# Mixing one chunk ahead in the output projection, an earlier priority for the last chunks of the FFN, and modulation weights loaded through GpSimd's queue

## The chip, the cores and the metric

The kernel is written in a tile framework for one NeuronCore of a Trainium2 chip. The core has TensorE (matrix products, PE in the profile), VectorE (DVE), ScalarE (ACT), GpSimd (POOL) and SyncE (SP), and 16 DMA engines. Each engine works through its own queue in order. DMAs are started by instructions in the queues of SP, POOL or ACT. The metric is the device time of one execution in microseconds; lower is better.

## The reference

One layer of a diffusion backbone on 1024 tokens of width 1024 with 256 context tokens, all float32:

```python
mod = silu(c) @ w_ada + b_ada                      # 6 x 1024: shift, scale, gate, twice
sh1, sc1, g1, sh2, sc2, g2 = split(mod, 6)
h = modulate(rmsnorm(x, norm1_g), sh1, sc1)
q, k, v, hv, hx1, hx2, gna, ghy = split(h @ w_in)  # 1024 -> 5120
y_na = neighbourhood_attention(q, k, v, k_ctx, v_ctx, rpb)
y_hy = hyena_mixer(hv, hx1, hx2, filters)          # long convolutions through FFTs
m = sigmoid(g_na) * (y_na @ w_na_o) + sigmoid(g_hy) * (y_hy @ w_hy_o)
x = x + g1 * (m @ w_out)
h2 = modulate(rmsnorm(x, norm2_g), sh2, sc2)
x = x + g2 * ((silu(h2 @ w1) * (h2 @ w3)) @ w2)    # hidden width 2816
return rmsnorm(x, final_g)
```

## The kernel before

Products keep float32 accuracy by splitting each operand into a high part in the matmul format (a ScalarE cast) and a low remainder (a VectorE subtraction); `split` (L175 and L176) makes both, and each product is the sum of three: low by high, high by low, high by high. `weights` (L178 to L185) loads a raw weight on SP and splits it.

The program is straight-line. The order of each engine's queue is set when the kernel is built: the framework walks the instructions by priority, which is program order unless a block stands under `high_priority`, and by when it estimates each to be ready. A tile of a pool with `bufs=n` has n places; a load into a place waits until the last reader of the tile that was there before is done.

The stages in order of time, by the names in the trace:

- 0 to 70 us: the early modulation (`ada_early`, L221 to L235), the norm and the turned hidden state `hT`.
- 70 to 280 us: the input projection (`project`, `in_ps`) interleaved with the filters of the Hyena branch and the late modulation. `filters` loads decay tiles `dec` on SP (L359, two places), multiplies them with `filt_ps` on VectorE (L370, `fv`), and transforms them (`dft_ps`, L442 to L444, with matrices `matf` loaded on SP). Spectra go to DRAM by SP (`spec<-ks`, L390) after a ScalarE copy. `ada_rows` (L870 to L921) computes the four late rows of the modulation on VectorE: for each of eight sums of 512 columns it takes eight tiles `wal` of 128x512 (64 loads of 256 KB, four places, L887) and accumulates them into `aacc` (L890, L892); a small matmul `ar_ps` adds over the partitions, and the rows go to DRAM by POOL (`mod<-arow`, L912). POOL's queue also carries the stores of projected tokens (`vtok`, `z`, `hx`, L572) and of projected rows (`qk`, L624), and at the start of each pair of rows eight small loads of the bias (L908).
- 280 to 800 us: the rest of the input projection with the convolutions. 800 to 920 us: attention with the Hyena output (`hyena_out`).
- 920 to 1062 us: `mix`. For each of eight chunks f of the merged channels it loads and splits the attention's output weight `wna[f]`, loads `wout[f]`, multiplies it by g1 and splits it into `wouh` and `woul`, computes `na_ps` for both halves of the tokens (24 matmuls), and on VectorE and ScalarE the gated sum and its split `mh` and `ml` (L1081 to L1084). After every second chunk `rows` (L1096) multiplies the two chunks with their output weights for all eight blocks of tokens (`out_ps`, L1107, 96 matmuls) and adds to the residual. The pool that holds `wouh`, `woul`, `mh` and `ml` has three places for each. The last two chunks are returned, and their `rows` run together with the second norm.
- 1062 to 1490 us: the FFN up, seven products in a Strassen scheme. 1490 to 1712 us: the FFN down, `ffn_down`: seven products of 11 chunks each, in the order 1, 2, 6, 5, 7, 3, 4; each chunk loads a 128x512 tile `ar<-g` (L1316) and splits it and a weight. `close` and `finish` (L1400 to L1431) end each block of the output. In product 4 the last `TAIL` = 3 chunks are multiplied together, block by block.

Of the kernel before, what the change touches and what calls it, by code (L numbers as in the profile page):

```python
# [158 lines left out]
class Block:  # L159
# [712 lines left out]
    def ada_rows(self, pool, psf):  # L872

        nc, a = self.nc, self.a
        ones = pool.tile([P, 32], F32, name="ones", tag="ones", bufs=1)
        nc.gpsimd.memset(ones, 1.0)

        def sums(r, pair):  # L880
            for n, part in enumerate(pair):
                for h in range(2):
                    acc = pool.tile([P, 512], F32, tag="aacc", name="aacc", bufs=2)
                    for k in range(8):
                        w = pool.tile([P, 512], F32, tag="wal2", name="wal", bufs=4)
                        at = part * D + 512 * h
                        nc.sync.dma_start(w, a["w_ada"][k, :, at:at + 512])  # L887
                        c = self.cs[:, 2 * k:2 * k + 1]
                        if k:
                            nc.vector.scalar_tensor_tensor(acc, w, c, acc, op0=ALU.mult, op1=ALU.add)  # L890
                        else:
                            nc.vector.tensor_scalar(acc, w, c, None, op0=ALU.mult)  # L892
                        yield 0.6
                    ps = psf.tile([P, 512], F32, tag="f", name="ar_ps")
                    for j in range(2):
                        g = 64 * h + 32 * j
                        nc.tensor.matmul(ps[g:g + 32, 0:256], ones, acc[:, 256 * j:256 * j + 256], start=True,
                                         stop=True, tile_position=(0, g))
                    rs = r[64 * h:64 * h + 64, 256 * n:256 * n + 256]
                    nc.vector.tensor_add(rs, ps[64 * h:64 * h + 64, 0:256], rs)  # L900

        for pair in ((3, 4), (2, 5)):
            r = pool.tile([P, 512], F32, tag="arow", name="arow", bufs=1)
            nc.gpsimd.memset(r, 0.0)
            for n, part in enumerate(pair):
                for j in range(4):
                    at = part * D + 256 * j
                    nc.gpsimd.dma_start(r[32 * j:32 * j + 1, 256 * n:256 * n + 256], a["b_ada"][0:1, at:at + 256])  # L908
            yield from sums(r, pair)
            for n, part in enumerate(pair):  # L910
                for j in range(4):
                    nc.gpsimd.dma_start(self.modd[part][0:1, 256 * j:256 * j + 256],  # L912
                                        r[32 * j:32 * j + 1, 256 * n:256 * n + 256])
            if pair[0] == 3:
                pt = psf.tile([P, 512], F32, tag="f", name="ada_t")
                for j in range(4):
                    nc.tensor.transpose(pt[:, j * P:(j + 1) * P], r[:, j * P:(j + 1) * P], self.ident)
                v = pt.rearrange("p (n h g q) -> p n q g h", n=2, h=2, g=4)[:, :, 0]
                cols = lambda t: t.rearrange("p (g h) -> p g h", h=2)
                nc.vector.tensor_copy(cols(self.mod2[:, 1, :]), v[:, 0])  # L920
                nc.vector.scalar_tensor_tensor(cols(self.mod2[:, 0, :]), v[:, 1], 1.0, cols(self.ng[:, 1, :]),  # L921
                                               op0=ALU.add, op1=ALU.mult)
# [139 lines left out]
    def mix(self, wp, wo, mp, psf, g1, x1):  # L1062

        nc, a = self.nc, self.a
        gs = []
        for f in range(8):
            wn = self.weights(wo, a["wna"][f], 512)
            raw = wp.tile([P, D], F32, tag="wor4", name="wor", bufs=2)
            nc.sync.dma_start(raw, a["wout"][f])
            nc.vector.tensor_tensor(raw, raw, g1, op=ALU.mult)  # L1070
            w = [mp.tile([P, D], F32R, tag=t, name=t) for t in ("wouh", "woul")]
            self.split(w[0], w[1], raw)
            m = [mp.tile([P, T], F32R, tag=t, name=t) for t in ("mh", "ml")]
            for h in range(2):
                sl = slice(h * 512, (h + 1) * 512)
                ps = psf.tile([P, 512], F32, tag="f", name="na_ps")
                self.gemm(ps, wn, self.ya, 4, 512, h * 512)
                ga = wp.tile([P, 2, 512], F32, tag="gate", name="gate")
                nc.sync.dma_start(ga[:, 0], self.gd[f][:, sl])
                nc.sync.dma_start(ga[:, 1], self.hyd[f][:, sl])  # L1080
                nc.scalar.activation(ga[:, 0], ga[:, 0], AF.Sigmoid)  # L1081
                nc.vector.tensor_tensor(ga[:, 0], ps, ga[:, 0], op=ALU.mult)
                nc.vector.tensor_add(ga[:, 0], ga[:, 0], ga[:, 1])
                self.split(m[0][:, sl], m[1][:, sl], ga[:, 0])  # L1084
            gs.append((m, w))
            if f == 1:
                for j in range(8):
                    nc.sync.dma_start(x1[j], a["x"][j * P:(j + 1) * P, :])
            if f == 7:
                return gs  # L1090
            if len(gs) == 2:
                for j in range(8):
                    self.rows(psf, x1[j], gs, j, "out_ps")
                gs = []

    def rows(self, psf, x1, gs, j, name):  # L1096

# [186 lines left out]
    def ffn_down(self, wa, pool, psf):  # L1284
# [5 lines left out]
        nc, a = self.nc, self.a  # L1290
        N = NH // 2
        AHEAD, TAIL = 4, 3
# [5 lines left out]
        def operand(src, early):  # L1298
            count[0] += not early
            return self.operand(wa if early or count[0] % 8 < 5 else _Bufs(pool, oh=3, ol=3), src)  # L1300

        def load(q, i, pin=True):
            sl = slice(512 * (q % 2), 512 * (q % 2) + 512)
            d = nc.sync.dma_start(w2[i][:, q, :], a["w2"][i + N * (q // 2)][:, sl])
            if pin:
                self.tc.keep_in_program_order(d)

        def product(n, ps, src, start, stop, loads=lambda i: ()):
            rest = []
            for i in range(N):  # L1310
                early = n == 1 and i < AHEAD
                ahead = ExitStack()
                if n != 1 and i == 0:
                    ahead.enter_context(self.tc.high_priority())
                x = wa.tile([P, 512], F32, tag="t", name="ar")
                d = nc.sync.dma_start(x, self.g2d[n][i])  # L1316
                if n == 1 and not early:
                    self.tc.keep_in_program_order(d)
                if early:
                    if i % 2 == 0:  # L1320
                        raw = wa.tile([P, D], F32, tag="wr", name="wr")
                    w = raw[:, 512 * (i % 2):512 * (i % 2) + 512]
                    nc.sync.dma_start(w, a["w2"][i][:, 0:512])
                else:
                    w = src(i)
                if n == 1 and i == AHEAD - 1:
                    for k in range(AHEAD, 2 * AHEAD):
                        load(0, k)
                for q, k, pin in loads(i):
                    load(q, k, pin)  # L1330
                rest.append((operand(x, early), operand(w, early)))
                ahead.close()
                if n == 4 and N - TAIL <= i < N - 1:
                    continue
                for j in range(4):
                    for k, (x, w) in enumerate(rest):
                        for c, (u, v) in enumerate(((1, 0), (0, 1), (0, 0))):
                            nc.tensor.matmul(ps[j], x[u][:, j * P:(j + 1) * P], w[v],  # L1338
                                             start=(start and i == 0 and c == 0),
                                             stop=(stop and i == N - 1 and k == len(rest) - 1 and c == 2),  # L1340
                                             skip_group_check=True)
                    if i == N - 1:
                        yield j
                rest = []
# [32 lines left out]
        for j in product(1, x, b11, True, False, lambda i: ((2, i - AHEAD, True),) if i >= AHEAD else ()):  # L1377
            nc.scalar.copy(c11[j], x[j])
# [6 lines left out]
        for j in product(6, x, t2, False, False):  # L1385
            nc.scalar.copy(c12[j], x[j])
# [83 lines left out]
```

## Time and profile before

| | |
|---|---|
| median of 3 runs | 1712.67 us (1707.35 to 1715.36) |
| the profiled execution | 1714.26 us, of which the span from the first to the last instruction is 1712.2 us |
| TensorE | busy 1655.7 us (97%), 8124 matmuls |
| VectorE | busy 1230.1 us (72%) |
| ScalarE | busy 662.3 us (39%) |
| GpSimd | busy 153.8 us (9%) |
| mean granted TensorE clock | 0.994 |

Busy times are unions of instruction spans. A wait is given as the idle time of an engine just before an instruction, with the instruction or DMA that ended it. A row of the timeline gives the start, the length, the engine (a q behind it stands for its queue), the line, the operation with out<-in, and how many followed each other.

### The profile page before, as it was taken

The page shows a single profiled execution, that of the slowest core. Times are in us where ns is not written, and L with a number is a line of the kernel's source. Part 1 is how long each engine was busy: PE and PEld are TensorE (multiplying, and loading weights), DVE is VectorE, ACT ScalarE, POOL GpSimd, SP SyncE. Part 2 cuts the span into 40 slices and gives each one's busy share as a digit, 9 for nine tenths or more (in the row PEclk, how much of TensorE's full clock was granted, in tenths as well). Part 3 has the DMA queues.
Part 4 walks back from the last instruction along what each step waited for, and adds up shares of the span by engine and source line. Part 5 has one row for each costly group of instructions (what it writes and reads, how often), then busy time and mean ns, then how long its engine had stood idle before and what let it go on. Part 6 is the DMA issues. An engine that isn't in the chain of part 4 may idle for free.

```text
span 1712.2 us, 22620 instructions
## 1 busy us (share of the span) xinstructions
PE 1655.7 (97%) x8124; PEld 1305.4 (76%) x8124; DVE 1230.1 (72%) x2076; ACT 662.3 (39%) x1141; POOL 153.8 (9%) x274
## 2 busy tenths in 40 slices
PE   6999998999999999999999999999999999999997
PEld 2676676777777778887787887888888888878886
DVE  3797586799995966465866868867865566479576
ACT  4611221322222224455654226733333333355455
POOL 0100210100010013020200001010101011100000
PEclk9999999999999999999999999999999999999999
DMA  9286854555463456354757425333433223395344
GB/s 363 101 267 196 272 179 151 203 158 180 156 222 137 138 202 193 104 150 135 215 163 251 140 68 184 123 123 117 156 103 109 95 99 108 106 384 174 99 121 154
DMA packets 114517, 282.48 MB, mean 165 GB/s; under 512 B 15839, under 2 KB 24675, under 8 KB 112101
## 3 DMA queue, kind: packets, MB, share of 16 engines
q1 hardware_dynamic: 94472, 219.99, 38.7%
q0 software_dynamic: 19280, 60.60, 10.5%
q8 instruction: 64, 1.05, 0.3%
q10 hardware_dynamic: 653, 0.44, 0.1%
q14 instruction: 48, 0.39, 0.1%
HBM read 213.60 MB, written 67.39 MB: 164 GB/s over the span
## 4 chain that ended last, share of the span: by engine, by line
PE 66%; issue 8%; DVE 4%; DMA 3%; ACT 1%; POOL 0%; SPq 0%; DVEq 0%; POOLq 0%; ACTq 0%
PE x_ps L1169 15%; PE in_ps L195 13%; PE z_ps L1169 7%; PE dx_ps L1338 5%; PE out_ps L1107 5%; PE dz_ps L1338 3%; PE dft_ps L442 2%; PE hy_ps L195 2%; PE y_ps L1169 2%; PE pt_ps L800 2%; PE pt_ps L786 2%; PE dft_ps L443 1%; PE dft_ps L444 1%; PE dy_ps L1338 1%; PE s_ps L766 1%
## 5 line engine op out<-in xcount | busy, mean ns | idle before, releaser
L195 PE MATMUL in_ps<-hTh,wl 128*128 128x512 f32 x640 | 258.9, 405 | 0.9 <-ACT proj L614 0.5
L195 PE MATMUL in_ps<-hTl,wh 128*128 128x512 f32 x640 | 253.4, 396 | 0.4 <-DVE hTl L176 0.2
L195 PE MATMUL in_ps<-hTh,wh 128*128 128x512 f32 x640 | 253.1, 396 | 0.0
L195 PEld LDWEIGHTS in_ps<-hTh,wl 128*128 128x128 f32 x640 | 121.0, 189 | 31.8 <-issue 5.6
L195 PEld LDWEIGHTS in_ps<-hTl,wh 128*128 128x128 f32 x640 | 121.1, 189 | 27.0 <-DVE hTl L176 1.9
L195 PEld LDWEIGHTS in_ps<-hTh,wh 128*128 128x128 f32 x640 | 121.0, 189 | 26.8 <-issue 0.4
L175 ACT CAST wh<-wr 128x1024 fp32r<-128x1024 f32 (+1 forms) x56 | 51.9, 926 | 140.9 <-PE in_ps L195 110.6
L176 DVE TENSOR_TENSOR wl<-wr,wh 128x1024 fp32r<-128x1024 f32 (+1 forms) x56 | 59.7, 1067 | 62.4 <-ACT wh L175 62.2
L176 DVE TENSOR_TENSOR ol<-ws,oh 128x512 fp32r<-128x512 f32 x88 | 60.4, 688 | 50.2 <-ACT oh L175 50.0
L176 DVE TENSOR_TENSOR ol<-ar,oh 128x512 fp32r<-128x512 f32 x77 | 52.8, 688 | 46.7 <-ACT oh L175 46.7
L175 ACT CAST oh<-ar 128x512 fp32r<-128x512 f32 x77 | 47.9, 622 | 83.5 <-PE dx_ps L1338 33.1
L175 ACT CAST oh<-ws 128x512 fp32r<-128x512 f32 x88 | 54.7, 622 | 56.6 <-PE x_ps L1169 26.5
L442 PE MATMUL dft_ps<-a,matf 128*128 128x512 f32 x128 | 66.3, 599 | 6.3 <-DVE a L430 4.3
L775 ACT ACTIVATE pe<-pe,mx 128x640 f32<-128x640 f32 x64 | 52.6, 822 | 49.1 <-DVE mx L774 49.1
L1338 PE MATMUL dx_ps<-ol,oh 128*128 128x512 f32 x176 | 68.7, 390 | 1.7 <-DVE ol L176 1.7
L774 DVE CUSTOM_DVE_ANT_0 pe<-s_ps,bias 128x640 f32<-128x640 f32 x64 | 50.1, 820 | 28.1 <-PE s_ps L769 28.1
L1338 PE MATMUL dx_ps<-oh,ol 128*128 128x512 f32 x176 | 67.3, 390 | 1.9 <-DVE ol L176 1.9
L1338 PE MATMUL dx_ps<-oh 128*128 128x512 f32 x176 | 68.5, 389 | 0.0
L176 DVE TENSOR_TENSOR ol<-wr,oh 128x512 fp32r<-128x512 f32 x70 | 48.0, 689 | 23.1 <-ACT oh L175 23.0
L175 ACT CAST oh<-wr 128x512 fp32r<-128x512 f32 x70 | 43.3, 622 | 52.7 <-PE x_ps L1169 17.3
L890 DVE SCALAR_TENSOR_TENSOR aacc<-wal,cs,aacc 128x512 f32<-128x512 f32 x56 | 41.8, 746 | 25.7 <-DMA wal<-in_w_ada 25.1
L1109 DVE TENSOR_TENSOR x<-x,out_ps 128x512 f32<-128x512 f32 x64 | 42.7, 684 | 18.6 <-PE out_ps L1107 18.3
(394 smaller groups left out, 4195.8 us busy)
## 6 DMA issues: line engine op xcount, KB each, us to landing
wr<-in_w SPq DMA_DIRECT2D x52, 512.0 KB, 3.4
wr<-in_w_in SPq DMA_DIRECT2D x40, 512.0 KB, 4.3
ar<-g SPq DMA_DIRECT2D x77, 256.0 KB, 2.9
wal<-in_w_ada SPq DMA_DIRECT2D x64, 256.0 KB, 4.4
matf<-in_dft_f SPq DMA_DIRECT2D x32, 384.0 KB, 5.0
bias<-in_rpb SPq DMA_DIRECT2D x64, 192.0 KB, 3.7
g<-t POOLq DMA_DIRECT2D x47, 256.0 KB, 3.1
w<-in_w SPq DMA_DIRECT2D x44, 256.0 KB, 5.4
```

What stands on the lines that cost most here:

```text
L175: self.nc.scalar.copy(hi, src)
L176: self.nc.vector.tensor_sub(lo, src, hi.bitcast(F32))
L195: mm = nc.tensor.matmul(ps, ww[:, k * P:(k + 1) * P], xx[:, k, pos:pos + width], start=(i == 0), stop=(i == n - 1))
L442: nc.tensor.matmul(ps, m[:, 0], v.rearrange("p a b -> p (a b)"), start=True, stop=False)
L774: nc.vector.tensor_tensor_reduce(pe, ps[:, 256:896], bt, -1.0, 3e38, ALU.add, ALU.min, mx[:, 0:1])
L775: nc.scalar.activation(pe, pe, AF.Exp, bias=mx[:, 0:1], scale=-1.0, accum_out=mx[:, 1:2])
L786: pin(nc.tensor.transpose(pt[:, at:at + P], pe[:, c * P:(c + 1) * P], self.ident))
L890: nc.vector.scalar_tensor_tensor(acc, w, c, acc, op0=ALU.mult, op1=ALU.add)
L1107: nc.tensor.matmul(ps, gg[x][:, tk], ww[y][:, sl], start=(i == 0), stop=(i == n - 1))
L1109: nc.vector.tensor_add(x1[:, sl], x1[:, sl], ps)
L1169: mm = nc.tensor.matmul(ps, w[u][:, k * P:(k + 1) * P], x[v][:, k, :], start=(start and k == 0 and i == 0), stop=(stop and k == 3 and i == 2),
L1338: nc.tensor.matmul(ps[j], x[u][:, j * P:(j + 1) * P], w[v], start=(start and i == 0 and c == 0), stop=(stop and i == N - 1 and k == len(re ...
```

## The change

Three places change. In `ada_rows` the 64 loads of `wal` are issued by GpSimd instead of SyncE. In `mix` the load and split of `wna[f + 1]` stand at the top of chunk f, and `rows` of two chunks runs when three chunks are ready, so behind the `na_ps` products of the third; the last two chunks are returned as before. In `ffn_down` the last three chunks of product 4 stand under `high_priority`, as the first chunk of each product after the first did already.

```diff
@@ ada_rows
-                        nc.sync.dma_start(w, a["w_ada"][k, :, at:at + 512])
+                        nc.gpsimd.dma_start(w, a["w_ada"][k, :, at:at + 512])
@@ mix
         gs = []
+        load = lambda f: self.weights(wo, a["wna"][f], 512) if f < 8 else None
+        after = load(0)
         for f in range(8):
-            wn = self.weights(wo, a["wna"][f], 512)
+            wn, after = after, load(f + 1)
             raw = wp.tile([P, D], F32, tag="wor4", name="wor", bufs=2)
...
             if f == 7:
                 return gs
-            if len(gs) == 2:
+            if len(gs) == 3:
                 for j in range(8):
-                    self.rows(psf, x1[j], gs, j, "out_ps")
-                gs = []
+                    self.rows(psf, x1[j], gs[:2], j, "out_ps")
+                gs = gs[2:]
@@ ffn_down, product
-                if n != 1 and i == 0:
+                if n != 1 and i == 0 or n == 4 and i >= N - TAIL:
                     ahead.enter_context(self.tc.high_priority())
```

## The prediction

> **What bounds the kernel now.** I read the page's first part, then the busy times in windows, then the chain of waits, then the waits by engine in each window that the change touches, and last the timeline around the longest of them.
>
> ```profile
> span 1712.2 us, 22620 instructions
> PE 1655.7 (97%) x8124; PEld 1305.4 (76%) x8124; DVE 1230.1 (72%) x2076; ACT 662.3 (39%) x1141; POOL 153.8 (9%) x274
> ```
>
> ```profile
> 70.00:272.00 202.00, 184.73 (x892) 137.72 (x890) 148.65 (x217) 44.59 (x79) 27.64 (x49) 0.97 0.70 228
> 138.80:145.60 6.80, 5.54 (x14) 3.98 (x15) 4.41 (x7) 0.00 (x0) 0.00 (x0) 0.50 0.80 260
> 261.70:268.50 6.80, 5.30 (x14) 3.79 (x15) 4.50 (x8) 0.00 (x0) 0.00 (x0) 0.50 0.68 226
> 915.00:1075.00 160.00, 154.08 (x717) 125.88 (x716) 118.28 (x172) 61.67 (x98) 5.17 (x9) 0.99 0.46 157
> 1640.00:1712.20 72.20, 62.91 (x276) 51.17 (x274) 53.44 (x96) 40.85 (x85) 0.00 (x0) 0.98 0.45 145
> ```
>
> The columns behind the length are PE, PEld, DVE, ACT, POOL, then granted clock, DMA share and GB/s. TensorE is the bound, and its work does not change: no matmul is added or removed. Only its idle time can move, 56.5 us of the span (1712.2 less 1655.7), and the stretches at half clock. Of the idle time 17.3 us lies in the window of the filters and the late modulation (202.0 less 184.7) and 5.9 us in that of the mix.
>
> **The mix.** Idle times before `rows` products, from the timeline of PE, and two chunks of `na_ps` in the chain of waits:
>
> ```profile
> 936.99 0.40 PE L1107 MATMUL out_ps<-wouh,mh 128*128 128x512 f32 x1
> 938.73 0.50 PE L1107 MATMUL out_ps<-wouh,ml 128*128 128x512 f32 x1 [1.34 <-DVE gate L1082]
> ...
> 969.07 0.39 PE L1107 MATMUL out_ps<-woul,mh 128*128 128x512 f32 x1
> 970.38 0.50 PE L1107 MATMUL out_ps<-wouh,ml 128*128 128x512 f32 x1 [0.92 <-DVE ml L176]
> ```
>
> ```profile
> 1034.08 0.40 PE L1107 MATMUL out_ps<-wouh,mh 128*128 128x512 f32 x1
> 1034.81 0.50 PE L1107 MATMUL out_ps<-wouh,ml 128*128 128x512 f32 x1 [0.33 <-DVE ml L176]
> ```
>
> ```profile
> 989.94 10.92 PE na_ps L195 x48
> ```
>
> A matmul follows the next after 10.92/48 = 0.23 us. From start to start the three waits take 1.74, 1.31 and 0.73 us, so they cost 1.51, 1.08 and 0.50. At each, PE has finished `na_ps` and stands until VectorE has made the second chunk's `ml`. With the change the 24 `na_ps` matmuls of a third chunk, 5.46 us, stand between. That covers the first two waits, which have less left than that. The last pair is still multiplied straight behind its own `na_ps`: the third wait stays. The gain is 1.51 + 1.08 = 2.6 us.
>
> The earlier load and split of `wna` moves eight 256 KB loads on SP past a `wout` and four gate loads each, and eight ScalarE and VectorE splits past a gated sum. They cost nothing: VectorE has 41.7 us free in that window (160.0 less 118.3), and PE now waits there for no `wl`. Without the cover one split would cost PE what a late `ml` costs now, at most 1.5 us. What is late next is the third place of `mh` and `wouh`: three chunks are now alive, so the splits of the next chunk wait for `rows` to end. If these don't fit into the 5.46 us, the waits come back. Bounds of this part: 3.1 us gained (all three) to 1.5 lost.
>
> **The loads of the late modulation.** Waits in 70 to 272 us, by PE, DVE, POOL and ACT:
>
> ```profile
> PE filt_ps L363 <- DVE fv L370: 9.5, 4, 3.8
> PE dft_ps L442 <- DVE a L430: 3.2, 3, 2.0
> ```
>
> ```profile
> DVE aacc L890 <- DMA wal<-in_w_ada: 25.1, 15, 4.7
> DVE fv L370 <- DMA dec<-in_decay: 18.3, 10, 3.6
> DVE aacc L892 <- DMA wal<-in_w_ada: 0.6, 1, 0.6
> ```
>
> ```profile
> POOL vtok L572 <- ACT tm L571: 59.1, 7, 15.7
> POOL mod L912 <- DVE arow L900: 47.1, 5, 26.8
> ```
>
> ```profile
> ACT tm L571 <- DMA vtok<-tm: 11.3, 4, 4.1
> ```
>
> VectorE waits 25.7 us for `wal` and 18.3 for `dec`, 44.0 together; PE waits 12.7 us for VectorE. So a microsecond of VectorE's DMA waits costs PE 12.7/44.0 = 0.29. Most of PE's time sits in two long waits. In the timelines of all engines around them:
>
> ```profile
> 133.05 0.32 SPq L390 DMA_DIRECT2D spec<-ks  x1
> 133.47 0.38 SPq L427 DMA_DIRECT2D matf<-in_dft_f  x1
> 133.94 0.90 SPq L359 DMA_DIRECT2D dec<-in_decay  x2
> 139.32 1.29 DVE L370 TENSOR_TENSOR fv<-filt_ps,dec 128x512 f32<-128x512 f32 x2 [3.15 <-DMA dec<-in_decay]
> ```
>
> ```profile
> 140.06 2.07 PE L363 MATMUL filt_ps<-fw,hid 64*128 64x256 f32 x6 [3.85 <-DVE fv L370]
> ```
>
> ```profile
> 254.49 0.48 DVE L892 TENSOR_SCALAR aacc<-wal,cs 128x512 f32<-128x512 f32 x1
> 255.00 0.33 SPq L887 DMA_DIRECT2D wal<-in_w_ada  x1
> 261.67 0.75 DVE L890 SCALAR_TENSOR_TENSOR aacc<-wal,cs,aacc 128x512 f32<-128x512 f32 x1 [4.34 <-DMA wal<-in_w_ada]
> 263.20 1.23 PE L363 MATMUL filt_ps<-fw,hid 64*128 64x256 f32 x4 [3.75 <-DVE fv L370]
> ```
>
> Each is followed by 6.8 us at half clock (the two window rows above). A long wait so costs 3.85 + 5.54/2 = 6.6 or 3.75 + 5.30/2 = 6.4 us, 6.5 in the mean, 13.0 for both. Neither hangs on the queue that issues `wal`. Ahead of the first, `dec` was issued behind a spectrum store and a matrix, not behind a `wal`, and took over 5 us to land. In the second, `wal` was issued 0.03 us after its place was freed (254.97), and the 6.6 us were the transfer. POOL's transfers were as slow then (the `vctok` store issued at 255.2):
>
> ```profile
> DMA to landing us min/median/max: 6.8/6.8/6.8
> ```
>
> The issue itself, on SP and on POOL, from the page of the tile `wal` and POOL's timeline:
>
> ```profile
> L887 SPq DMA_DIRECT2D wal<-in_w_ada x64: 327/382/1497, 76.5 to 264.6; - x64
> ```
>
> ```profile
> 76.51 1.47 POOL L908 DMA_DIRECT2D arow<-in_b_ada  x3 [0.29 <-POOL arow L904]
> 79.32 2.40 POOL L908 DMA_DIRECT2D arow<-in_b_ada  x5
> ```
>
> ```profile
> 191.24 0.75 DVE L890 SCALAR_TENSOR_TENSOR aacc<-wal,cs,aacc 128x512 f32<-128x512 f32 x1 [2.24 <-DMA wal<-in_w_ada]
> 194.47 2.12 SPq L887 DMA_DIRECT2D wal<-in_w_ada  x4
> 200.54 0.75 DVE L890 SCALAR_TENSOR_TENSOR aacc<-wal,cs,aacc 128x512 f32<-128x512 f32 x1 [4.71 <-DMA wal<-in_w_ada]
> ```
>
> - Removed from SP: 64 issues of 0.38 us, 24 us that SP has to spare, and the standing behind other SP work. The load at 194.47 went out 2.5 us after its place was freed (191.24 + 0.75), about half of the 4.71 us that VectorE then waited; that at 255.00 lost nothing. Between none and half I take a third: 8.6 of the 25.7 us.
> - Added on POOL: a POOL DMA starts 0.29 us after its release and takes 0.48 (2.40/5), 0.39 more than SP's 0.38. On the 16 waits that is 6.2 us.
> - Added once: program order puts the eight bias loads, 3.9 us, ahead of the first `wal`.
> - Behind a waiting `wal` on POOL stand the token and row stores; their buffers are waited for by ScalarE (11.3 us now), and so by the eviction of `in_ps`. I price that in the rivals.
>
> The sum is -8.6 + 6.2 + 3.9 = +1.5 us on VectorE, times 0.29: 0.4 us lost on PE. The bounds are 13.0 gained, when both long waits go, and 13.0 lost, when as many come. I take 0.4, since the two rows that carry the time name transfers and not a queue.
>
> [...]
>
> **The tail of the FFN.**
>
> ```profile
> 1677.97 1.07 PE L1338 MATMUL dx_ps<-oh,ol 128*128 128x512 f32 x4
> 1680.77 0.50 PE L1338 MATMUL dx_ps<-ol,oh 128*128 128x512 f32 x1 [1.73 <-DVE ol L176]
> ```
>
> This is the only wait of product 4: 1.73 us, by the order of the matmuls in its third chunk, not in the last three. I take 0 for the priority. It can be 1.7 gained if the order shifts, or 2.7 lost, one chunk's 12 matmuls, if the hoisted splits take places that nearer chunks need. The splits and loads hoisted are twelve instructions and three DMAs that run anyway.
>
> **Sum.** -2.6 + 0.4 + 0 = -2.2 us. The profiled execution, 1714.26 us (the span and 2.1 around it), becomes 1712.1. It stands 1.6 above the median of the runs, 1712.67; against that median the forecast is 1710.5.
>
> **Rivals.**
>
> One or both long waits of the filters go, because loads on POOL no longer share SP's queue with `dec`, `matf` and the spectra. For it: SP holds all of these, and `dec` on a less loaded queue would be earlier. Against it: the second wait was pure transfer. It gives 1704.0 with one gone and 1697.5 with both. [...]
>
> Slower: a `wal` stands on POOL behind a store that waits for ScalarE, or a store behind a `wal`. POOL stood 59.1 us for `tm` and 47.1 us for `arow`; a `wal` behind a 15.7 us wait would starve VectorE's next accumulation, and PE behind it. Against it: POOL was otherwise empty then, and the loads may be ordered ahead of those stores. Each additional long wait costs 6.5: 1717.0 with one, 1723.5 with two, from which on it is a slowdown beyond 0.5%.
>
> The mix gains nothing, because the third place binds and the waits return elsewhere: 1713.1.
>
> **How the numbers follow.** A measurement here can tell about 0.5%, 8.6 us, from no change: below 1704.1 or above 1721.2. The forecast has a chance of 0.38 and its own range is 1706 to 1714; long waits go 0.26 (both 0.1, one 0.16, of which half falls under the bound, the mix included); long waits come 0.24 (two or more 0.18); the mix gains nothing 0.12. Of the forecast's 0.38, 0.08 lie under the bound, where mix and tail reach their lower bounds and some short waits of the filters go too. Faster is so 0.1 + 0.08 + 0.08 = 0.26, slower 0.18, same 0.56. The range reaches from both waits gone, 1697, to two more, 1724.
>
> **What would show it.** Right: PE's waits before `rows` fall from three to one of about 0.3 us; the half-clock stretches in 70 to 272 us stay two; VectorE's waits for `wal` stay near 25 us and those for `dec` near 18; the wait in product 4 stays. The prediction is wrong if the window of the filters ends earlier or later by more than 6 us, which the number of half-clock stretches shows, or if POOL's waits move onto `wal` loads and PE's waits for `in_ps` evictions appear.

## The result, and the profile after

The changed kernel takes 1727.87 us in the median of 6 runs (1724.91 to 1729.31), the kernel before 1714.06 beside it (1707.35 to 1716.03): a ratio of 1.0083, 95% interval 1.0065 to 1.0101, or 14 us slower (11 to 17). The forecast was 1710.5 with a range up to 1724. The profiled execution took 1726.39 us, 11.0 us more of span than before. First the page of the changed kernel:

```profile
span 1723.2 us, 22611 instructions
PE 1658.3 (96%) x8124; PEld 1307.8 (76%) x8124; DVE 1230.4 (71%) x2076; ACT 662.4 (38%) x1141; POOL 187.6 (11%) x338
```

The work is the same; TensorE is idle 64.9 us instead of 56.5. To see where, I take one stretch that holds the same 972 matmuls in every kernel, from TensorE's 247th to its 1219th: the stage of the filters and the late modulation. The columns behind the length are PE, PEld, DVE, ACT and POOL busy, then granted clock, DMA share and GB/s. Before:

```profile
70.44:290.07 219.63, 202.22 (x973) 151.83 (x973) 160.73 (x232) 48.50 (x84) 29.22 (x51) 0.97 0.66 217
```

After, with the stretch around its longest wait as the second row:

```profile
70.51:301.04 230.53, 205.61 (x972) 154.20 (x973) 161.38 (x232) 48.43 (x84) 63.62 (x115) 0.96 0.63 207
269.70:279.95 10.25, 6.32 (x16) 4.62 (x17) 5.72 (x9) 0.00 (x0) 1.84 (x4) 0.50 0.69 239
```

The stage is 10.9 us longer, which is the whole loss of this execution. TensorE's idle time in it went from 17.4 (219.63 less 202.22) to 24.9 us; the other 3.4 us are longer matmuls at the lower clock (202.22 to 205.61 busy): at clock 0.50 one `in_ps` matmul followed the last after 0.43 us, from 147.42 to 149.98, and at 1.00 after 0.23, from 150.59 on. The half-clock stretches went from two, of 6.8 us each, to four, of 20.5 us together (the last section has them). Only POOL has gained work. TensorE's longest waits, from its view by engine in 70 to 291 us of the changed kernel; before, the four rows were 9.5, 0.4, 3.2 and 1.4 us:

```profile
PE filt_ps L363 <- DVE fv L370: 13.3, 5, 6.3
PE dft_ps L442 <- issue: 3.2, 2, 2.0
PE dft_ps L442 <- DVE a L430: 2.6, 2, 1.8
PE dft_ps L442 <- DMA matf<-in_dft_f: 2.6, 1, 2.6
```

So 3.8 of the 7.5 us of added idle time stand at the filters' products, and nearly as much, 3.4, at the transforms `dft_ps`, most of it without a releaser that the profile shows ("issue"). VectorE's waits, in the same view:

```profile
DVE fv L370 <- DMA dec<-in_decay: 20.3, 11, 4.2
DVE aacc L890 <- DMA wal<-in_w_ada: 20.3, 12, 7.3
DVE wl L176 <- ACT wh L175: 16.0, 3, 9.2
...
DVE aacc L892 <- DMA wal<-in_w_ada: 1.0, 1, 1.0
```

VectorE waits *less* for DMAs than before, 41.6 us (20.3 + 20.3 + 1.0) against 44.0, and TensorE loses all the same: fewer waits, but the longest for `wal` grew from 4.7 to 7.3 us. In the median the loads on POOL land no later than on SP. The last line of the view of the tile `wal`, after; before it was 2.9/4.4/6.2:

```profile
DMA to landing us min/median/max: 2.8/4.2/7.1
```

What a load stands behind in its queue, and the order that the planner makes of it, is what the runs below found.

**A load behind a waiting store.** The longest wait, in the timelines of POOL, VectorE and TensorE after:

```profile
265.14 0.71 POOL L572 DMA_DIRECT2D vctok<-tm  x1 [3.74 <-ACT tm L571]
265.87 0.52 POOL L912 DMA_DIRECT2D mod<-arow  x1
266.41 0.58 POOL L887 DMA_DIRECT2D wal<-in_w_ada  x1
```

```profile
261.93 0.49 DVE L892 TENSOR_SCALAR aacc<-wal,cs 128x512 f32<-128x512 f32 x1
262.45 2.33 DVE L890 SCALAR_TENSOR_TENSOR aacc<-wal,cs,aacc 128x512 f32<-128x512 f32 x3
272.11 0.75 DVE L890 SCALAR_TENSOR_TENSOR aacc<-wal,cs,aacc 128x512 f32<-128x512 f32 x1 [7.33 <-DMA wal<-in_w_ada]
```

```profile
273.63 2.07 PE L363 MATMUL filt_ps<-fw,hid 64*128 64x256 f32 x6 [6.25 <-DVE fv L370]
```

The place for the load at 266.41 was free at 262.42, when VectorE's step of 261.93 ended. POOL stood meanwhile at the store of `vctok`, whose tile ScalarE had not made yet, and passed it at 265.14. So the load went out 4.0 us late; VectorE stood 7.33 us, TensorE 6.25, and the stretch of 10.25 us around it ran at clock 0.50. The wait itself is not new: before, the same load held VectorE for 4.34 us and TensorE for 3.75, with 6.8 us at half clock.

**VectorE's order.** Neither kernel fixes this order by hand. VectorE around 130 us, before:

```profile
127.88 2.32 DVE L890 SCALAR_TENSOR_TENSOR aacc<-wal,cs,aacc 128x512 f32<-128x512 f32 x3
131.57 1.29 DVE L370 TENSOR_TENSOR fv<-filt_ps,dec 128x512 f32<-128x512 f32 x2 [1.38 <-PE filt_ps L363]
```

And after, with TensorE behind it:

```profile
130.60 1.53 DVE L890 SCALAR_TENSOR_TENSOR aacc<-wal,cs,aacc 128x512 f32<-128x512 f32 x2
134.51 0.75 DVE L890 SCALAR_TENSOR_TENSOR aacc<-wal,cs,aacc 128x512 f32<-128x512 f32 x1 [2.38 <-DMA wal<-in_w_ada]
137.23 0.75 DVE L890 SCALAR_TENSOR_TENSOR aacc<-wal,cs,aacc 128x512 f32<-128x512 f32 x1 [1.96 <-DMA wal<-in_w_ada]
138.54 0.75 DVE L890 SCALAR_TENSOR_TENSOR aacc<-wal,cs,aacc 128x512 f32<-128x512 f32 x1 [0.56 <-DMA wal<-in_w_ada]
139.21 1.28 DVE L370 TENSOR_TENSOR fv<-filt_ps,dec 128x512 f32<-128x512 f32 x2
```

```profile
139.95 1.59 PE L363 MATMUL filt_ps<-fw,hid 64*128 64x256 f32 x4 [2.44 <-DVE fv L370]
```

Before, three accumulations and then the filters' product `fv`, for which TensorE waits (2.44 us at 139.95 in the changed kernel). After, two accumulations, then three that wait 4.9 us for their loads (2.38 + 1.96 + 0.56), and only then the product. Counted along VectorE's queue, 21 accumulations stood ahead of this product before and 23 after; ahead of the second filter's sums (L378) it was 27 before and 32 after.

**The mix and the tail.** TensorE's waits from 915 to 1085 us, after:

```profile
PE hT_ps L1140 <- DVE x L1122: 3.1, 3, 2.0
PE pt_ps L800 <- ACT yrow L807: 1.5, 1, 1.5
PE na_ps L195 <- ACT yrow L807: 0.4, 1, 0.4
```

No `out_ps` wait is left: the 1.34, 0.92 and 0.33 of before are all gone. In the tail nothing moved; the wait of 1.73 us in product 4 is still there.

### The profile page after: what moved, and what is told of

Its sections match the earlier page's. It is cut to its first block, busy times and chain, and to the rows that moved or that the text cites. A ratio compares the mean times of both kernels' runs of the same rounds, so it can differ in the third digit from the quotient of the medians.

```text
span 1723.2 us, 22611 instructions
## 1 busy us (share of the span) xinstructions
PE 1658.3 (96%) x8124; PEld 1307.8 (76%) x8124; DVE 1230.4 (71%) x2076; ACT 662.4 (38%) x1141; POOL 187.6 (11%) x338
## 4 chain that ended last, share of the span: by engine, by line
PE 42%; issue 29%; DVE 5%; POOL 3%; DMA 3%; ACT 1%; SPq 0%; POOLq 0%; DVEq 0%; ACTq 0%
PE in_ps L195 9%; PE dx_ps L1340 6%; PE out_ps L1109 4%; PE dz_ps L1340 3%; PE x_ps L1171 3%; PE na_ps L195 2%; PE hy_ps L195 2%; PE dft_ps L442 2%; PE pt_ps L800 2%; PE pt_ps L786 2%; PE dy_ps L1340 1%; POOL g L1284 1%; PE s_ps L766 1%; PE dft_ps L443 1%; PE dft_ps L444 1%
## 5 line engine op out<-in xcount | busy, mean ns | idle before, releaser
L890 DVE SCALAR_TENSOR_TENSOR aacc<-wal,cs,aacc 128x512 f32<-128x512 f32 x56 | 41.8, 747 | 21.2 <-DMA wal<-in_w_ada 20.3
```

## Experiments

All ratios are to the kernel before, run beside it on the same chip; microseconds are the ratio's. The chip is one for E1 to E4, E16 and E17, another for E5 to E7, a third for E8 to E11 and a fourth for E12 to E15. Where runs of different chips are compared, as E5 with E8 to E12, E9 with E12, E12 and E13 with E16 and E17, or E3 with E14 and E15, that rests on the ratios.

**The parts alone.** E1 is the kernel before with the change to L887 only; E2 the changed kernel without it; E3 only the diff in `mix`; E4 only the line in `ffn_down`.

```diff
-                        nc.sync.dma_start(w, a["w_ada"][k, :, at:at + 512])
+                        nc.gpsimd.dma_start(w, a["w_ada"][k, :, at:at + 512])
```

> The kernel before with its 64 late modulation loads on GpSimd, the mix and the tail as before. Theory A (the loads alone make the loss): the trace of the changed kernel is 10.96 us behind by the end of the filters (291.18 against 280.22) and 11.0 at its end, with the mix and the tail giving back about 1.1 and 0 in between, so this kernel should be 11 to 12.5 us slower than before, with the filters' milestone near 291. Rival B (the parts need each other, since the planner deals the order anew): well under 9 us slower.

> The changed kernel with the 64 loads back on SyncE. Theory A: the filters' milestone back at 280, and the kernel 0.5 to 2.6 us faster than before. Rival B: still several us slower than before.

> The mix one chunk ahead alone. By the prediction's step 2.6 us faster than before; by the milestones of the changed kernel's trace (the lag goes from 12.0 us at the start of the mix to 10.9 at the last transpose of the second norm) 1.1 faster, the rest given back where PE waits 2.03 us for the second norm's chunk. Rival: no gain, 0.

> The priority of the FFN's tail alone. By the prediction's step 0; the wait of 1.73 us in product 4 stays. Rival: 1.7 faster, or up to 2.7 slower.

| | ratio | 95% interval | us |
|---|---|---|---|
| E1 loads alone | 1.0110 | 1.0092 to 1.0128 | +18.8 |
| E2 mix and tail | 0.9983 | 0.9968 to 0.9998 | -2.9 |
| E3 mix alone | 0.9982 | 0.9969 to 0.9994 | -3.1 |
| E4 tail alone | 1.0001 | 0.9987 to 1.0016 | +0.2 |

The whole loss comes with the loads, and the mix and the tail do what the prediction said. E1 is slower than expected by 6 to 8 us; its engines work in the same order as the changed kernel up to the mix, and its stage in the profiled execution was 4.4 us longer still:

```profile
70.80:305.72 234.92, 206.91 (x972) 154.67 (x973) 161.46 (x232) 48.30 (x84) 63.75 (x115) 0.94 0.62 203
```

So the same instructions in the same order spread by several microseconds from execution to execution in this stage (E1's runs go from 1727.68 to 1736.34, and its profile is of the slowest), and a single profile's stage length is no measurement of a few microseconds. In E3's profile TensorE's waits in the mix are

```profile
PE hT_ps L1140 <- DVE x L1122: 1.4, 3, 0.9
```

so the 2.0 us wait of the changed kernel there was one execution's, not the mix's. The tail's wait of 1.7 us stands in E4 as before.

**Queue or order.** Moving the loads to POOL lets the planner deal the stage anew: 106 places in VectorE's queue, 46 in TensorE's and 39 in SyncE's hold another instruction than before (the loads themselves left out); ScalarE's is unchanged. E5 takes the loads on POOL with the old order, E6 the loads on SP with the new one. Both add edges of order, without semaphores, from a list for each engine:

```diff
+def keep(tc, nc):
+    by = {i.name: i for i in nc.cur_bb.bb.instructions}
+    for names in ORDER:          # one list for each engine, the stage's instructions
+        for a, b in zip(names, names[1:]):
+            tc.add_manual_dep(by[f"I-{b}"], f"I-{a}", ..., reason="order")   # ...: class NoSync
```

> The 64 loads on GpSimd, as in the kernel with the loads alone, but PE, VectorE, ScalarE and SyncE (without those loads) take their instructions in the order they had in the kernel before: edges of order alone, no waits added. Only the queue of the loads is changed. Theory A (the queue: places on POOL that come late, its slower issue, transfers that collide): 15 to 20 us slower, as with the loads alone. Theory B (the order: the planner takes the loads on GpSimd to be early and deals VectorE's accumulations ahead of the filters' products, 32 against 27 of them before the second filter's sums, and PE's matmuls in another order): within 4 us of before.

> The mirror: the loads on SyncE as before, and PE, VectorE, ScalarE and SyncE (without those loads) in the order that they have in the kernel with the loads alone on GpSimd. Theory A: within 4 us of before. Theory B: 12 to 20 us slower.

E5: 1.0096 (1.0066 to 1.0126), +16. E6: 1.0089 (1.0066 to 1.0113), +15. Each alone costs about as much as both together (E1): neither theory holds by itself, and the costs do not add. E6 is no clean test of VectorE's order. With the loads back on SP they stood there ahead of the decay loads: SyncE waited for a place of `wal` until 81.00, and issued `dec` only after that. SyncE's timeline in E6:

```profile
81.00 0.33 SPq L887 DMA_DIRECT2D wal<-in_w_ada  x1
...
82.33 1.12 SPq L359 DMA_DIRECT2D dec<-in_decay  x2
```

E5 is clean, as only the queue differs from before. Its early loss, in POOL's and VectorE's timelines:

```profile
79.16 2.87 POOL L908 DMA_DIRECT2D arow<-in_b_ada  x6
82.03 1.79 POOL L887 DMA_DIRECT2D wal<-in_w_ada  x3
```

```profile
80.39 0.48 DVE L892 TENSOR_SCALAR aacc<-wal,cs 128x512 f32<-128x512 f32 x1
86.18 0.75 DVE L890 SCALAR_TENSOR_TENSOR aacc<-wal,cs,aacc 128x512 f32<-128x512 f32 x1 [5.31 <-DMA wal<-in_w_ada]
86.85 1.28 DVE L370 TENSOR_TENSOR fv<-filt_ps,dec 128x512 f32<-128x512 f32 x2
```

The second `wal` left behind the bias loads, and the filters' product stood behind its accumulation. At the end a load waited behind the store of `vctok` as in the changed kernel, and TensorE 5.87 us.

**Half the loads.** E7 issues only those of the first pair on POOL.

```diff
-                        nc.sync.dma_start(w, ...)
+                        (nc.gpsimd if pair[0] == 3 else nc.sync).dma_start(w, ...)
```

> Only the first 32 of the loads (the pair of parts 3 and 4, up to about 190 us) on GpSimd, the other 32 on SyncE. By the milestones the lag is 9 of 11 us at 200 us in the changed kernel and 12 of 15.7 with the loads alone, so 9 to 13 us slower if the places add up; the rest would be the load that stood behind a waiting token store at 266.41. Rival: if the whole loss hangs on the last long wait, 2 to 4.

1.0056 (1.0035 to 1.0078), +9.6: the loss is spread over both pairs, as the first theory said.

**What stands ahead in the queue.** All with the loads on POOL. E8 to E10 keep the old order: E8 issues the bias loads on SP, E9 the stores of `vtok` and `vctok` on ScalarE behind the copy that makes them, E10 does both. E11 is the changed kernel, in its own order, with both.

```diff
-                    nc.gpsimd.dma_start(r[32 * j:32 * j + 1, ...], a["b_ada"][0:1, at:at + 256])
+                    nc.sync.dma_start(r[32 * j:32 * j + 1, ...], a["b_ada"][0:1, at:at + 256])
...
-            nc.gpsimd.dma_start(dst[:, 4 * h:4 * h + m], st[:, :m])
+            (by or nc.gpsimd).dma_start(dst[:, 4 * h:4 * h + m], st[:, :m])   # by: nc.scalar for vtok, vctok
```

> The 64 loads on GpSimd with the order of before kept on the other engines, and the 16 bias loads issued by SyncE, so that none stands ahead of a load of the modulation on GpSimd. Theory A1 (bias loads ahead): in the trace with them on GpSimd the second load went out at 82.03 behind them, VectorE stood 5.31 us for it and PE 3.58 at 87.59, and the lag was 3.6 us by 90; the second group stood before load 45 (VectorE 5.19), and the lag grew by 2.8 between 220 and 240. So 4 to 6.5 us less lag at 250 than there, and about 11 us slower than before instead of 16. Rival: the loads are late for another reason, no change.

> The same order and queue, bias loads on GpSimd, but the stores of the token tiles of the value chunks (vtok, vctok) issued by ScalarE, which makes them, so that GpSimd does not stand for them. Theory A2 (a load behind a waiting store): load 60 was free at 261.6 and went out at 266.65 behind the store of 265.44, VectorE stood 7.47 and PE 5.87 with 10.2 us at half clock after it; the load now goes out near 262, the wait falls to 2 to 4 us and 3 to 5 us are won. Rival: the transfer is as late anyway, since the 16 DMA engines are shared: no change.

> Both edits. If A1 and A2 are the queue's whole cost and add: 5 to 8 us slower than before at most, perhaps none. If a loss of 10 us or more stays, the cost lies in the transfers and not in what stands ahead of them in the queue.

> The changed kernel (mix and tail with it, and the planner's own order) with both edits. If only the queue counted: the loss of 14 us gone, with the mix's 2 to 3 us on top: 0 to 3 us faster than before. If the new order counts by itself, as the mirror run says: still 6 to 12 us slower.

| | ratio | 95% interval | us |
|---|---|---|---|
| E5 old order, nothing moved | 1.0096 | 1.0066 to 1.0126 | +16.4 |
| E8 bias loads on SP | 1.0067 | 1.0052 to 1.0082 | +11.5 |
| E9 token stores on ScalarE | 1.0062 | 1.0047 to 1.0077 | +10.6 |
| E10 both | 1.0041 | 1.0029 to 1.0053 | +7.0 |
| E11 both, planner's order | 1.0088 | 1.0071 to 1.0105 | +15.0 |

E8 and E9 alone overlap with E5 in their intervals; together (E10) they are clear of it. E9's trace shows its mechanism beside E5's: the load in question went out as its place came free, VectorE waited 4.78 us instead of 7.47 and TensorE 2.30 instead of 5.87. E9's VectorE and TensorE:

```profile
268.19 0.75 DVE L890 SCALAR_TENSOR_TENSOR aacc<-wal,cs,aacc 128x512 f32<-128x512 f32 x1 [4.78 <-DMA wal<-in_w_ada]
```

```profile
269.72 1.65 PE L363 MATMUL filt_ps<-fw,hid 64*128 64x256 f32 x5 [2.30 <-DVE fv L370]
```

E8 and E10 moved the bias loads ahead of something else: in E10 SyncE issues five of them and only then the decay loads, and VectorE waits 5.67 us for one of those. The early loss did not shrink there, against what I expected. SyncE and VectorE in E10:

```profile
80.61 1.48 SPq L908 DMA_DIRECT2D arow<-in_b_ada  x5
82.19 0.83 SPq L359 DMA_DIRECT2D dec<-in_decay  x2
```

```profile
88.33 0.69 DVE L370 TENSOR_TENSOR fv<-filt_ps,dec 128x512 f32<-128x512 f32 x1 [5.67 <-DMA dec<-in_decay]
```

E11 says that with the planner's order the same edits win nothing. But the planner deals a new order for each choice of queues: 15 accumulations stand ahead of the first filter's sums in E11, 7 in the changed kernel and 5 before. The changed kernel's own order with E11's queues was not run.

**Late bias loads, and whose order it is.** E12 has the old order, the token stores on ScalarE, and the bias loads on POOL again but behind the first loads of their pair. E13 is the same in the planner's order (a new one again, with 13 accumulations ahead of the first filter's sums); E16 keeps VectorE's order alone, E17 SyncE's alone.

```diff
-                    nc.gpsimd.dma_start(r[...], a["b_ada"][...])     # in ada_rows, ahead of sums
+                    if n + h == 0: ...                               # the same eight, in sums, ahead of the first ar_ps
```

> The loads on GpSimd, the order of before kept on the other engines, the token stores on ScalarE, and the bias loads on GpSimd again but traced behind the first eight loads of their pair, so that four to six loads go out ahead of them and SyncE has none. Theory (what stands ahead in a queue is the cost): the 6.5 us lost by 90 us with the bias loads on SyncE fall to 2 or less, and the kernel is 0 to 3 us slower than before. Rival (the transfers themselves collide): still 6 to 8 us slower.

> The same queues as the run before, but the planner's own order. Theory (the order counts by itself): 8 to 15 us slower than before, at least 5 more than the run with the order kept. Rival (only the queues count): the same as that run.

> Late bias loads, token stores on ScalarE, the loads on GpSimd, and VectorE alone kept in the order of before; SyncE stays in the planner's order but for 7 places, PE moves with VectorE but for 16. Theory (VectorE's accumulations ahead of the filters' products are the order's cost): like the run with all orders kept, about 5 us slower than before, filter stage 218 to 222 us. Rival (SyncE's order): like the run with the planner's order, about 11 slower, stage 225 to 228.

> The same with SyncE alone kept in the order of before; VectorE and PE stay close to the planner's order (10 and 32 accumulations ahead of the first and second sums). Theory (VectorE): about 11 us slower than before, stage 225 to 228. Rival (SyncE): about 5 slower, stage 218 to 222.

| same queues in all four | ratio | 95% interval | us |
|---|---|---|---|
| E12 all orders old | 1.0027 | 1.0009 to 1.0045 | +4.6 |
| E16 VectorE's order old | 1.0036 | 1.0020 to 1.0051 | +6.2 |
| E13 planner's order | 1.0063 | 1.0041 to 1.0086 | +10.8 |
| E17 SyncE's order old | 1.0074 | 1.0048 to 1.0099 | +12.7 |

E12 differs from E9 only in the place of the bias loads, and is clear of it (4.6 us against 10.6). Times follow VectorE's order: the two kernels that keep it lose 5 to 6 us, the two that don't 11 to 13. The intervals of E12 and E13, and of E16 and E17, overlap at the edge, so the four together carry this, not one pair. TensorE moved with VectorE in E16, so the two aren't separated. The stage lengths that I had expected of E16 and E17 were not met: E16's profile shows 227.5 us, but that execution was the slowest of its twelve (1713.82 to 1723.01); E12's shows 219.8, and was the fastest of its twelve (1711.83 to 1724.15).

**A better version?** E14 is E12 with the mix as well; E15 the mix alone with `dec` at 3 places and `wal` at 3.

```diff
-                        dec.append(pool.tile([P, 512], F32, tag="dec", name="dec", bufs=2))
+                        dec.append(pool.tile([P, 512], F32, tag="dec", name="dec", bufs=3))
...
-                        w = pool.tile([P, 512], F32, tag="wal2", name="wal", bufs=4)
+                        w = pool.tile([P, 512], F32, tag="wal2", name="wal", bufs=3)
```

> The run with late bias loads and the order kept, with the mix one chunk ahead as well. If the queue costs nothing there: 2 to 3 us faster than before, the same as the mix alone. To beat the mix alone it would need more than 4.

> The mix alone, loads on SyncE, with one place moved from the modulation's weights (4 to 3) to the decay (2 to 3). If VectorE's 18 us of waits for decay loads count as much as its 25 for the weights: no difference to the mix alone, 3 us faster than before. If a late decay load is what starts the long waits of PE (3.85 at 140.06 was one): one of them goes, 6 more. If the weights are the tighter: 5 to 10 slower than the mix alone.

E14: 1.0009 (0.9995 to 1.0024). E15: 0.9987 (0.9973 to 1.0000). Neither is shown to beat the mix alone, 0.9982, which is about 3 us faster than before with the loads left on SP: E14 is clear of it on the slow side, and E15 overlaps with it.

## Why the prediction was wrong, step by step

- **The mix, -2.6 us: right.** E3 measured 3.1 us (1.0 to 5.3). All three `out_ps` waits went, not two: the third, which was said to stay, is gone too, so the bound of 3.1 fits the trace better; why the third went was not looked into, and the interval can't tell 2.6 from 3.1. What was named as late next, the third place, did not bind: TensorE has no wait left there.
- **The tail, 0: right.** E4 measured +0.2 us (-2.2 to 2.7).
- **The loads, +0.4 us: wrong; E1 measured 18.8 (15.8 to 21.9),** beyond even the bound of 13.0. Four things in that step failed.
- *"-8.6 + 6.2 + 3.9 = +1.5 us on VectorE, times 0.29".* The sum itself was off by 3.9 us, on the side of a gain: VectorE's DMA waits fell by 2.4, from 44.0 to 41.6 us in the changed kernel. Its reason held: of the 60 `wal` loads that have to wait for a place, 24 went out more than 1 us after it was free before, and 12 after. The conversion was wrong. TensorE's waits for VectorE rose from 12.7 to 15.9 us (13.3 + 2.6) while VectorE's fell, and with its other waits and the lower clock the stage lost 10.9 us. The ratio 0.29 is an average over the waits of one order; which instruction stands behind a wait decides. In E5 one late load held up a product of the filters for 5.31 us, and at the end a 7.33 us wait cost TensorE 6.25 in the changed kernel.
- *The order of the queues.* The working took the order of VectorE, TensorE and SyncE as fixed. In this framework the order is made from estimates of when things are ready, so a load's queue is an input to it. With equal queues the planner's order cost 6 us more than the old one (E13 against E12), and E16 and E17 put that on the side of VectorE, with TensorE that moved with it.
- *"Added once: program order puts the eight bias loads, 3.9 us, ahead of the first `wal`", so 1.1 us on TensorE.* They come twice, once for each pair, and stood ahead of the loads that VectorE needed first. E8 is 5 us under E5 and E9 6, both with overlapping intervals; E10's two edits won 9, and E12's, which put the bias loads behind, 12, both clear of E5.
- *"Behind a waiting `wal` on POOL stand the token and row stores ... I price that in the rivals".* This rival, loads behind a waiting store, had a chance of 0.24 and is what happened at 266.41, with the 7.33 us wait; it lengthened a long wait that was there before, rather than adding one. Its counter-argument ("POOL was otherwise empty then") overlooked that POOL, however little else it held, stood 3.74 us at the store of `vctok` and issued the load behind it 4.0 us late.
- **"POOL's waits move onto `wal` loads"** was named as a sign of a wrong prediction, and is there: POOL waits 47.6 us for VectorE's accumulations before a load. TensorE's waits for `in_ps` evictions, named beside it, did not come. The sign of the filter window (more than 6 us later) came true as well, with four half-clock stretches where two were to stay.
- **Settled in part:** what of the 4.6 us of E12 (1.5 to 7.7) is left on POOL. At one place the decay loads landed later in the run that issued the `wal` loads sooner. E5 and E12 have the order of before on all engines but POOL (in E12 ScalarE also issues the token stores). In E5, where the bias loads held the `wal` loads back, one `wal` was out when SyncE issued two decay loads at 79.91; in E12 four were out when it issued the same two at 80.31. Before, with two out, VectorE used them 4.8 us after their issue at 80.06 (84.84). From issue to landing they took, in E5 and then in E12:

```profile
DMA to landing us min/median/max: 4.1/4.2/4.2
DMA to landing us min/median/max: 6.4/6.8/7.2
```

VectorE's waits moved from one kind of load to the other. In E12 they are, against 18.3 and 25.1 us before:

```profile
DVE fv L370 <- DMA dec<-in_decay: 26.7, 9, 4.7
DVE aacc L890 <- DMA wal<-in_w_ada: 15.3, 8, 3.4
```

The later landing is seen at one place, in one execution of each kernel. That the `wal` loads cause it, or that it makes up the whole of the 4.6 us, is not shown. VectorE's new order with SyncE's old one and the loads on SP, which would have been the clean mirror, was not tried.

## What to carry to other kernels

When a load moves to another queue, write down for each of its issues what stands ahead of it in the new queue and what that waits for; in the changed kernel one store that waited for ScalarE sent the load behind it out 4.0 us late. Ask too which loads of other queues are out at the same time: the two decay loads landed after 4.2 us in the median beside one `wal` load (E5) and after 6.8 beside four (E12). Where the build deals the order of the engines from estimates, compare the two orders before costing anything, since a changed queue is also a changed order. And don't turn waits of an engine off the critical path into time by a mean ratio: look which instruction of the critical path stands behind each of them.

## What the runs showed of the hardware

In the changed kernel's trace a `wal` load on POOL started 0.29 to 0.30 us after VectorE freed its place in 44 of the 60 loads that wait for one, and took 0.54 us to issue (536 ns in the median, 582 at most); on SP, in the trace of before, the least was 0.03 us, and the issue took 382 ns in the median. The loads landed 4.2 us after their issue in the median on POOL, and 4.4 on SP.

The half clock came after short waits too. In the changed kernel's trace, between 70 and 300 us, the clock was 0.50 from 140.04 to 143.45, 146.87 to 150.28, 194.65 to 198.07 and 269.75 to 279.99 us: three times for 3.41 us and once for 10.24. The starts lie whole multiples of 3.41 us apart, and the windows below are stretches of that length, counted from them. Two waits of about 2 us in TensorE's timeline, the two windows that hold the first, the window that holds the second, and the one behind it:

```profile
86.39 0.49 PE L363 MATMUL filt_ps<-fw,hid 64*128 64x256 f32 x2 [2.19 <-DVE fv L370]
...
145.77 1.13 PE L363 MATMUL filt_ps<-fw,hid 64*128 64x256 f32 x6 [1.99 <-DVE fv L370]
```

```profile
82.02:85.43 3.41, 2.19 (x16) 1.72 (x14) 0.00 (x0) 0.46 (x1) 2.40 (x5) 1.00 0.90 322
85.43:88.84 3.41, 2.45 (x12) 1.83 (x13) 3.14 (x4) 0.86 (x2) 0.54 (x1) 1.00 1.05 385
143.45:146.87 3.42, 1.43 (x9) 0.72 (x7) 2.21 (x4) 0.00 (x0) 0.75 (x2) 1.00 0.85 297
146.87:150.27 3.40, 3.40 (x9) 2.72 (x9) 2.76 (x5) 0.00 (x0) 1.61 (x3) 0.50 0.84 269
```

The longer wait, 2.19 us, is spread over two windows, which leaves TensorE busy for 2.19 and 2.45 us of them (the first number behind the length), and the clock stayed at 1.00. The shorter one, 1.99 us, lies in one window, which leaves 1.43, and the next 3.4 us ran at clock 0.50 although TensorE was busy throughout. Between those 70 and 300 us of this trace, and of that of the kernel before, the clock fell after each of the six windows at full clock with 1.99 us or more of idle time, and after none with 1.82 or less; at 1070.61 in the trace of before it fell after a window with 1.42. These are counts from one execution of each kernel: no run varied the idle time alone, and no limit is shown.
